# A decoder block with split fp32r weights: on-chip pools in another order, stationary high tiles 64 bytes into their slots

## The chip, the cores and the metric

The kernel runs on one core of a Trainium2 chip. The metric is device time of one execution in microseconds (us), lower is better; a profile beside it shows one execution instruction by instruction. PE is TensorE's matmul, PEld its weight load, DVE VectorE, ACT ScalarE, POOL GpSimd, SP SyncE.

## The reference

One decoder layer over 256 tokens of width 2048, all in float32: a SwiGLU feed-forward, a mixer (a gated linear recurrence beside dilated attention), a second SwiGLU, each with layer norm behind it, and a gated per-layer embedding at the end.

```python
x = layer_norm(ALPHA * x + 0.5 * swiglu(x, ffn1_w_gate, ffn1_w_up, ffn1_w_down), ln1_g, ln1_b)
mix = hybrid_mixer(x, positions, w_in, conv_w, ..., lru_lambda, w_out)
x = layer_norm(ALPHA * x + mix, ln2_g, ln2_b)
x = layer_norm(ALPHA * x + 0.5 * swiglu(x, ffn2_w_gate, ffn2_w_up, ffn2_w_down), ln3_g, ln3_b)
x = x + sigmoid(x @ w_ple_gate) * (p @ w_ple_proj)
```

## The kernel before

Weights arrive in chunks of 256 rows by 512 columns (128 partitions, two k-halves of 512, 512 KB). `make_plan` lists them in the order in which the products take them. SP loads a chunk into a `raw` tile, ACT rounds it into a `hi` tile (line 86), DVE writes the rest `raw - hi` into a `lo` tile (line 92). There are nine hi slots and nine lo slots of 4096 bytes a partition, and preparation runs up to seven chunks ahead. Activations are split in the same way; the layer's input stands transposed in `xT`, for each of 16 blocks `kb` 256 tokens of the high part and then 256 of the low part. A product is hi*hi + lo*hi + hi*lo, all through the helper `mm` (line 203). Three kinds of it fill PE, in program order:

- Gate, up and channel products (`tokens_a`, `mm_stationary_w`): the weight is stationary. For each 128x128 block of a chunk there is a pair of matmuls: the hi block with 512 columns of `xT` (both parts), then the lo block with 256 columns (the high part). A chunk has 8 pairs, a group of eight chunks 64. At the two places where a layer norm of the second token half is still due, the group runs per token half, with 256 and 128 columns.
- Down and output products (`down_mm`): the activation, in a tile of the `work` pool, is stationary; hi, lo and hi again of the weight stream past as 512 columns, in triples.
- Value, query/key and ple-gate products (`tokens_b`): the same triples with `xT` as the stationary operand. The last quarter of the ple gate (`group_b_last`) streams 256 columns for the second token half.

The first three chunks of each of three stages lie in `work` tiles instead of slots (`e["work"]`).

Each tile's place follows from the order of the pools in `build`: const (`xT`, acc, identity and tables), small, raw, hi, lo, work, work1, qk. Const takes 53,888 bytes of a partition and small 576; the raw, hi, lo and work tiles are all 4096 bytes long.

Of the kernel before, what the change touches and what calls it, by code (L numbers as in the profile page):

```python
# [6 lines left out]
F32R = mybir.dt.float32r  # L7
# [5 lines left out]
P = 128  # L13
# [5 lines left out]
QW, KVW, LRU = 1536, 512, 1536  # L19
C_X = QW + 2 * KVW  # L20
C_Y = C_X + LRU
# [9 lines left out]
MAGIC = 12582912.0  # L31
AHEAD = 7
SLOTS = 9
PI_IN = 3.1415925


class Block:
# [17 lines left out]
    def bank(self):  # L55
        return self.tile(self.psum, [P, 512], F32, "mm")

# [1 line left out]
    def split(self, hi, lo, src, pool=False):  # L59
        self.nc.scalar.copy(hi, src)  # L60
        (self.nc.gpsimd if pool else self.nc.vector).tensor_tensor(lo, src, hi.bitcast(F32), op=ALU.subtract)  # L61

# [1 line left out]
    def load(self, q):  # L64
        e = self.plan[q]
        if e.get("load"):
            e["load"]()
        e["raw"] = self.tile(self.wraw, [P, 2, 512], F32, "raw")
        for k in e["parts"]:
            self.nc.sync.dma_start(e["raw"][:, k, :], e["src"][:, k, :])  # L70

    def prepare_hi(self, q):
        while self.loaded < min(len(self.plan), q + 4):
            self.load(self.loaded)
            self.loaded += 1
        e = self.plan[q]
        if e.get("split"):
            e["split"]()
        if e["work"]:
            e["hi"], e["lo"] = self.wide_r((P, 2, 512)), self.wide_r((P, 2, 512))  # L80
        else:
            e["hi"] = self.tile(self.whi, [P, 2, 512], F32R, "hi")
            e["lo"] = self.tile(self.wlo, [P, 2, 512], F32R, "lo")
            self.live += 1
        for k in e["parts"]:
            self.nc.scalar.copy(e["hi"][:, k, :], e["raw"][:, k, :])  # L86
# [7 lines left out]
    def advance(self, need=0):  # L94
        end = min(self.limit, self.taken + AHEAD)
        while self.ready < end and (self.plan[self.ready]["work"] or self.live < SLOTS):
            self.prepare_hi(self.ready)
# [44 lines left out]
    def make_plan(self):  # L142
        i = self.i
        plan = self.plan = []

        def add(w, r0, c0, n=1, **kw):
            for j in range(n):
                plan.append({"src": self.rows2(w, r0 + 256 * j, c0), "work": False, "pool": False,
                             "parts": [slice(0, 2)], **kw})

        def ffn(name):
            g, u, d = (i[f"{name}_w_{v}"] for v in ("gate", "up", "down"))
            for c in range(NCH):
                add(g, 0, c * 512, 8)
                add(u, 0, c * 512, 8)
                if c:
                    down(d, (c - 1) * 512)
            down(d, (NCH - 1) * 512)

        def down(w, r0):  # L160
            for n in range(4):
                add(w, r0, n * 512, 2)

        w, wo = i["w_in"], i["w_out"]
        ffn("ffn1")
        for j in range(8):
            plan[j]["load"] = lambda j=j: self.load_x(j)
            plan[j]["split"] = lambda j=j: self.split_x(j)
            plan[16 + j]["load"] = lambda j=j: self.load_acc(j)
        plan[0]["parts"] = [slice(0, 1), slice(1, 2)]  # L170
        v0 = len(plan)
        add(w, 0, QW + KVW, 8)
        for g in range(3):
            add(w, 0, C_X + g * 512, 8)
        for h in range(4):
            add(w, 0, h * 512, 8)
        for g in range(3):
            add(w, 0, C_Y + g * 512, 8)
            down(wo, g * 512)
        down(wo, 3 * 512)  # L180
        f0 = len(plan)
        ffn("ffn2")
        p0 = len(plan)
        for n in range(4):
            add(i["w_ple_proj"], 0, n * 512)
        for n in range(4):
            add(i["w_ple_gate"], 0, n * 512, 8)
        for q in (v0, f0, p0):
            for e in plan[q:q + 3]:
                e["work"] = e["pool"] = True  # L190
        plan[p0]["load"], plan[p0]["split"] = self.load_p, self.split_p
        self.xraw = {}
        self.limit = len(plan)
        self.loaded = self.ready = self.ready_lo = self.taken = self.live = 0
        self.ticks = 0
        self.lru_q, self.att_q, self.gate_q, self.res_q = [], [], [], []
# [1 line left out]
    def rows2(self, w, r0, c0):  # L198
        return w[r0:r0 + 256, c0:c0 + 512].rearrange("(k p) c -> p k c", p=P)

# [1 line left out]
    def mm(self, out, lhsT, rhs, start, stop):  # L202
        self.nc.tensor.matmul(out, lhsT=lhsT, rhs=rhs, start=start, stop=stop, skip_group_check=True)  # L203

# [148 lines left out]
        for e in es[3]:  # L353
            self.done(e)

# [1 line left out]
    def ln_stats(self, st, t, n):  # L357
        self.nc.vector.bn_stats(st[:, n, :], self.acc[:, t, n * 512:(n + 1) * 512])  # L358

# [38 lines left out]
                nc.gpsimd.tensor_tensor(a, a, gb[:, 1, :], op=ALU.add)  # L398
                yield

# [1 line left out]
    def swiglu(self, boundary):  # L402
        nc = self.nc
        pend = None
        for c in range(NCH):
            gate = []

            def on_gate(b, bank):
                g = self.narrow()
                self.evac_a(bank, g)  # L410
                s = self.narrow()
                nc.scalar.activation(s, g, AF.Sigmoid)  # L412
                nc.vector.tensor_tensor(g, g, s, op=ALU.mult)  # L413
                gate.append(g)

            self.group_a(on_gate, boundary and c == 0)
            if c == 1 and not boundary:
                self.res_q.append(self.tables())
            ah, al = self.wide_r(), self.wide_r()

            def on_up(b, bank):
                u = self.narrow()
                self.evac_a(bank, u)
                nc.vector.scalar_tensor_tensor(u, gate[b], 0.5, u, op0=ALU.mult, op1=ALU.mult)  # L424
                self.split(ah[:, b, :], al[:, b, :], u)

            self.group_a(on_up)
            if pend is not None:
                self.down(pend, c == 1)
            pend = (ah, al)  # L430
        self.down_last(pend)

# [1 line left out]
    def setup(self):  # L434
        nc, i = self.nc, self.i
        c = self.const
        self.ident = c.tile([P, P], F32, name="ident")
        make_identity(nc, self.ident)
        self.mhalf = c.tile([P, 1], F32, name="mhalf")
        nc.gpsimd.memset(self.mhalf, -0.5)  # L440
        self.par = c.tile([P, 192], F32, name="par")
        self.trig = c.tile([P, 2, 2, 16], F32, name="trig")
        self.dec = c.tile([P, 2, 12], F32, name="dec")
# [11 lines left out]
    def rope_table(self):  # L455
# [13 lines left out]
        for n, part in enumerate(TWO_PI_PARTS):  # L469
            nc.vector.scalar_tensor_tensor(r, k, -part, r if n else ang, op0=ALU.mult, op1=ALU.add)  # L470
        nc.vector.tensor_scalar(r, r, PI_IN, -PI_IN, op0=ALU.min, op1=ALU.max)
        nc.scalar.activation(self.trig[:, 1], r, AF.Sin)
# [23 lines left out]
        nc.vector.tensor_scalar(self.dec[:, 0, :], h, -8.0, None, op0=ALU.mult)  # L496
        nc.vector.tensor_scalar(self.dec[:, 1, :], h, -4.0, None, op0=ALU.mult)

# [1 line left out]
    def lru(self, g, xb):  # L500
        nc, i = self.nc, self.i
        wg = self.wide((P, 2, 4, P))
# [61 lines left out]
        yield  # L564
        nc.vector.tensor_tensor(al, q, ah.bitcast(F32), op=ALU.subtract)

# [1 line left out]
    def attention(self, h, qks):  # L568
        nc = self.nc
        for t in range(2):  # L570
# [58 lines left out]
        yield  # L629
        nc.vector.tensor_tensor(self.att[1][:, h, :], ob[:, :256], self.att[0][:, h, :].bitcast(F32), op=ALU.subtract)  # L630

# [1 line left out]
    def channels(self):  # L633
        got = []

# [38 lines left out]
            act = rec  # L674
        self.down_last(act)

# [1 line left out]
    def ple_proj(self):  # L678
        nc, i = self.nc, self.i
        for n in range(4):  # L680
# [51 lines left out]
    def build(self):  # L732
        tc = self.tc
        with (
            tc.tile_pool(name="const", bufs=1) as self.const,
            tc.tile_pool(name="small", bufs=2) as self.small,
            tc.tile_pool(name="wraw", bufs=5) as self.wraw,
            tc.tile_pool(name="whi", bufs=SLOTS) as self.whi,
            tc.tile_pool(name="wlo", bufs=SLOTS) as self.wlo,
            tc.tile_pool(name="work", bufs=12) as self.work,  # L740
            tc.tile_pool(name="work1", bufs=6) as self.work1,
            tc.tile_pool(name="qkp", bufs=3) as self.qk,
            tc.tile_pool(name="psum", bufs=8, space=bass.MemoryType.PSUM) as self.psum,
            tc.manual_schedule(),
        ):
            self.xT = self.const.tile([P, KB, 2, S], F32R, name="xT")
            self.acc = self.const.tile([P, 2, D], F32, name="acc")
            self.make_plan()
            self.setup()
            self.which = 0  # L750
            self.swiglu(False)
            self.mixer()
            self.swiglu(True)
            self.ple_proj()
            self.ple_gate()
# [44 lines left out]
```

## Time and profile before

| what | value |
|---|---|
| median of three runs | 1959.88 us (1959.28 to 1960.81) |
| span of the profiled execution | 1958.6 us |
| PE busy | 1946.0 us, 99% |
| PEld busy | 1665.9 us, 85% |
| DVE, ACT busy | 1293.7 us (66%), 962.3 us (49%) |
| matmuls | 10244 |
| granted TensorE clock | 1.000 throughout |
| DMA | 375.27 MB, mean 192 GB/s |

A matmul's listed duration runs from its start to a modelled end and overlaps the next one's; what one costs in a dense stream is the distance from its start to the next start. In the timeline a row is a run of equal instructions, so the hi and the lo matmul of a pair have a row each, and a triple has one row for lo and one for two hi's.

### The profile page before, as it was taken

The numbers are of one execution on the slowest core, as the hardware profiler recorded it, in microseconds if no ns is written. First come the engines' busy times: TensorE is split into PE (matmuls) and PEld (weight loads), VectorE is DVE, ScalarE is ACT, GpSimd is POOL, SyncE is SP. The second block draws the span as 40 slices with busy tenths as digits, with TensorE's granted clock in tenths as the row PEclk, the third lists the DMA queues.
The fourth block names the chain that finished last, engine by engine and source line by source line (L and its number), as shares of the span: only waits on it lengthen the run. The fifth ranks groups of instructions, "written<-read, shape, count | busy, mean of one in ns | idle before, by whom it ended". The sixth has DMA issues, their size and how long they took to land.

```text
span 1958.6 us, 26578 instructions
## 1 busy us (share of the span) xinstructions
PE 1946.0 (99%) x10244; PEld 1665.9 (85%) x10244; DVE 1293.7 (66%) x1679; ACT 962.3 (49%) x1330; POOL 151.2 (8%) x93
## 2 busy tenths in 40 slices
PE   8999999999999999999999999999999999999999
PEld 7888888888888888888888898888888888888787
DVE  6667565656665666778677786566556656565875
ACT  6544444444444446656754545444444444444552
POOL 0000000000000012301100250000000000000151
PEclk9999999999999999999999999999999999999999
DMA  9666565556655665655456466656565656655563
GB/s 315 206 210 201 166 218 190 174 171 215 205 176 177 193 205 183 226 163 171 141 193 194 150 207 222 195 172 219 168 214 173 195 169 217 193 173 172 178 223 132
DMA packets 195007, 375.27 MB, mean 192 GB/s; under 512 B 11953, under 2 KB 14657, under 8 KB 194881
## 3 DMA queue, kind: packets, MB, share of 16 engines
q1 hardware_dynamic: 193856, 370.42, 58.4%
q0 software_dynamic: 1024, 3.16, 0.5%
q8 instruction: 80, 1.31, 0.3%
q14 instruction: 47, 0.38, 0.1%
HBM read 371.43 MB, written 2.10 MB: 191 GB/s over the span
## 4 chain that ended last, share of the span: by engine, by line
PE 99%; DVE 1%; DMA 0%; issue 0%; ACT 0%; SPq 0%; POOL 0%; DVEq 0%
PE mm L203 98%; PE mm L380 1%; DVE w L61 0%; DMA raw<-in_ffn_w_gate_dram 0%; DVE lo L92 0%; PE mm L586 0%; DVE bst L358 0%; DVE acc L315 0%; ACT hi L86 0%; POOL rs L367 0%; DVE acc L370 0%; SPq L70 0%; DVE qk L698 0%; PE mm L619 0%; PE mm L618 0%
## 5 line engine op out<-in xcount | busy, mean ns | idle before, releaser
L203 PE MATMUL mm<-xT,hi 128*128 128x512 f32 (+1 forms) x3216 | 1121.3, 393 | 6.2 <-DVE xT L61 5.3
L86 ACT CAST hi<-raw 128x1024 fp32r<-128x1024 f32 (+1 forms) x676 | 693.4, 1048 | 620.7 <-PE mm L203 423.3
L92 DVE TENSOR_TENSOR lo<-raw,hi 128x1024 fp32r<-128x1024 f32 (+1 forms) x676 | 839.5, 1280 | 231.6 <-ACT hi L86 230.1
L203 PE MATMUL mm<-xT,lo 128*128 128x256 f32 (+1 forms) x3216 | 899.1, 280 | 0.0
L203 PEld LDWEIGHTS mm<-xT,hi 128*128 128x128 f32 x3216 | 606.0, 188 | 143.6 <-ACT hi L86 6.4
L203 PEld LDWEIGHTS mm<-xT,lo 128*128 128x128 f32 x3216 | 604.1, 188 | 1.7 <-DVE lo L92 0.8
L203 PE MATMUL mm<-hi,w 128*128 128x512 f32 x1672 | 521.6, 390 | 0.0
L203 PEld LDWEIGHTS mm<-hi,w 128*128 128x128 f32 x1672 | 313.9, 188 | 65.4
L203 PE MATMUL mm<-lo,w 128*128 128x512 f32 x836 | 325.5, 389 | 0.6 <-DVE lo L92 0.6
L308 DVE TENSOR_TENSOR w<-mm,w 128x256 f32<-128x256 f32 x200 | 83.4, 419 | 194.7 <-ACT w L307 194.6
L203 PEld LDWEIGHTS mm<-lo,w 128*128 128x128 f32 x836 | 157.0, 188 | 32.7 <-DVE lo L92 1.0
L203 PE MATMUL mm<-hi,xT 128*128 128x512 f32 (+1 forms) x584 | 180.2, 385 | 0.0
L315 DVE TENSOR_TENSOR acc<-acc,mm 128x512 f32<-128x512 f32 x184 | 122.1, 681 | 63.2 <-PE mm L203 63.2
L92 POOL TENSOR_TENSOR w<-raw,w 128x1024 fp32r<-128x1024 f32 x9 | 25.9, 2911 | 1318.7 <-ACT w L86 679.8
L307 ACT COPY w<-mm 128x256 f32<-128x256 f32 x200 | 72.5, 365 | 112.3 <-PE mm L203 112.3
L203 PEld LDWEIGHTS mm<-hi,xT 128*128 128x128 f32 x584 | 107.2, 188 | 23.1
L203 PE MATMUL mm<-lo,xT 128*128 128x512 f32 (+1 forms) x292 | 111.4, 382 | 0.0
L60 ACT CAST w<-w 128x256 fp32r<-128x256 f32 x90 | 36.5, 407 | 92.3 <-DVE w L424 92.3
L61 DVE TENSOR_TENSOR w<-w,w 128x256 fp32r<-128x256 f32 x90 | 43.2, 481 | 41.9 <-ACT w L60 41.9
L413 DVE TENSOR_TENSOR w<-w,w 128x256 f32<-128x256 f32 x88 | 39.0, 444 | 44.2 <-ACT w L412 44.2
L203 PEld LDWEIGHTS mm<-lo,xT 128*128 128x128 f32 x292 | 54.8, 188 | 11.1
L412 ACT ACTIVATE w<-w 128x256 f32<-128x256 f32 x88 | 36.8, 418 | 48.6 <-DVE w L308 48.5
(125 smaller groups left out, 624.6 us busy)
## 6 DMA issues: line engine op xcount, KB each, us to landing
raw<-in_ffn_w_up_dram SPq DMA_DIRECT2D x176, 512.0 KB, 4.7
raw<-in_ffn_w_down_dram SPq DMA_DIRECT2D x176, 512.0 KB, 4.8
raw<-in_ffn_w_gate_dram SPq DMA_DIRECT2D x175, 512.0 KB, 4.6
raw<-in_w_in_dram SPq DMA_DIRECT2D x88, 512.0 KB, 4.5
raw<-in_w_out_dram SPq DMA_DIRECT2D x32, 512.0 KB, 4.6
raw<-in_w_ple_gate_dram SPq DMA_DIRECT2D x32, 512.0 KB, 4.9
w<-in_ln_g_dram SPq DMA_DIRECT2D x12, 256.0 KB, 9.0
w<-in_ln_b_dram SPq DMA_DIRECT2D x12, 256.0 KB, 7.9
```

The source lines that it names most:

```text
L60: self.nc.scalar.copy(hi, src)
L61: (self.nc.gpsimd if pool else self.nc.vector).tensor_tensor(lo, src, hi.bitcast(F32), op=ALU.subtract)
L86: self.nc.scalar.copy(e["hi"][:, k, :], e["raw"][:, k, :])
L92: eng.tensor_tensor(e["lo"][:, k, :], e["raw"][:, k, :], e["hi"][:, k, :].bitcast(F32), op=ALU.subtract)
L203: self.nc.tensor.matmul(out, lhsT=lhsT, rhs=rhs, start=start, stop=stop, skip_group_check=True)
L307: self.nc.scalar.copy(c, bank[:, 256:])
L308: self.nc.vector.tensor_tensor(dst, bank[:, :256], c, op=ALU.add)
L315: self.nc.vector.tensor_tensor(a, a, bank, op=ALU.add)
L380: nc.tensor.transpose(bank[:, q * P:(q + 1) * P], self.acc[:, t, kb * P:(kb + 1) * P], self.ident)
L412: nc.scalar.activation(s, g, AF.Sigmoid)
L413: nc.vector.tensor_tensor(g, g, s, op=ALU.mult)
```

## The change

The pools stand in another order: raw, hi, lo, work, const, small, work1, qk. A hi slot becomes 4352 bytes long; a chunk whose plan entry is marked `stationary` (gate, up, the x and y channels) begins 64 bytes into its slot, every other at the slot's start. Lo tiles, raw tiles and work tiles keep their size. The instructions, their order, shapes, waits and DMAs stay as they are. Removed comments are left out here.

```diff
+LINE = 16
...
         else:
-            e["hi"] = self.tile(self.whi, [P, 2, 512], F32R, "hi")
+            o = LINE if e["stationary"] else 0
+            e["hi"] = self.tile(self.whi, [P, 1024 + 4 * LINE], F32R, "hi")[:, o:o + 1024].rearrange("p (k c) -> p k c", k=2)
             e["lo"] = self.tile(self.wlo, [P, 2, 512], F32R, "lo")
...
-                             "parts": [slice(0, 2)], **kw})
+                             "parts": [slice(0, 2)], "stationary": False, **kw})
...
-                add(g, 0, c * 512, 8)
-                add(u, 0, c * 512, 8)
+                add(g, 0, c * 512, 8, stationary=True)
+                add(u, 0, c * 512, 8, stationary=True)
...
-            add(w, 0, C_X + g * 512, 8)
+            add(w, 0, C_X + g * 512, 8, stationary=True)
...
-            add(w, 0, C_Y + g * 512, 8)
+            add(w, 0, C_Y + g * 512, 8, stationary=True)
...
         with (
-            tc.tile_pool(name="const", bufs=1) as self.const,
-            tc.tile_pool(name="small", bufs=2) as self.small,
             tc.tile_pool(name="wraw", bufs=5) as self.wraw,
             tc.tile_pool(name="whi", bufs=SLOTS) as self.whi,
             tc.tile_pool(name="wlo", bufs=SLOTS) as self.wlo,
             tc.tile_pool(name="work", bufs=12) as self.work,
+            tc.tile_pool(name="const", bufs=1) as self.const,
+            tc.tile_pool(name="small", bufs=2) as self.small,
             tc.tile_pool(name="work1", bufs=6) as self.work1,
```

## Rows read from the trace of the kernel before

**Rows 1.** The page: an engine's busy time, share, instructions; then the chain's shares by engine.

```profile
PE 1946.0 (99%) x10244; PEld 1665.9 (85%) x10244; DVE 1293.7 (66%) x1679; ACT 962.3 (49%) x1330; POOL 151.2 (8%) x93
PE 99%; DVE 1%; DMA 0%; issue 0%; ACT 0%; SPq 0%; POOL 0%; DVEq 0%
```

**Rows 2.** Waits of PE: who waited for whom, us in total, times, longest.

```profile
PE mm L203 <- DVE xT L61: 5.3, 1, 5.3
PE mm L380 <- DVE acc L370: 1.5, 1, 1.5
PE mm L203 <- ACT hi L86: 0.9, 1, 0.9
PE mm L203 <- DVE lo L92: 0.6, 1, 0.6
```

**Rows 3.** Groups by shape: count | busy us, mean modelled ns | idle before, releaser.

```profile
L203 PE MATMUL mm<-xT,hi 128*128 128x512 f32 x3136 | 1102.3, 395 | 6.2 <-DVE xT L61 5.3 <-ACT hi L86 0.9
...
L203 PE MATMUL mm<-hi,w 128*128 128x512 f32 x1672 | 521.6, 390 | 0.0
...
L203 PE MATMUL mm<-hi,xT 128*128 128x512 f32 x520 | 169.3, 399 | 0.0
...
L203 PE MATMUL mm<-lo,xT 128*128 128x512 f32 x260 | 102.6, 395 | 0.0
...
L203 PE MATMUL mm<-xT,hi 128*128 128x256 f32 x80 | 19.1, 335 | 0.0
...
L203 PE MATMUL mm<-xT,w 128*128 128x256 f32 x48 | 11.4, 335 | 0.0
...
L203 PE MATMUL mm<-w,xT 128*128 128x512 f32 x36 | 8.9, 399 | 0.0
```

**Rows 4.** Timeline of PE, pairs behind a down stage: start, length (us), instruction.

```profile
123.82 0.28 PE L203 MATMUL mm<-xT,lo 128*128 128x256 f32 x1
...
124.17 0.28 PE L203 MATMUL mm<-xT,lo 128*128 128x256 f32 x1
...
157.66 0.28 PE L203 MATMUL mm<-xT,lo 128*128 128x256 f32 x1
```

**Rows 5.** Timeline of PE, pairs in the first group.

```profile
19.75 0.28 PE L203 MATMUL mm<-xT,lo 128*128 128x256 f32 x1
...
54.37 0.28 PE L203 MATMUL mm<-xT,lo 128*128 128x256 f32 x1
```

**Rows 6.** Timeline of PE, the first down triples behind pairs, and later ones.

```profile
166.74 0.39 PE L203 MATMUL mm<-lo,w 128*128 128x512 f32 x1
...
168.12 0.39 PE L203 MATMUL mm<-lo,w 128*128 128x512 f32 x1
...
172.20 0.39 PE L203 MATMUL mm<-lo,w 128*128 128x512 f32 x1
...
186.48 0.39 PE L203 MATMUL mm<-lo,w 128*128 128x512 f32 x1
```

**Rows 7.** Timeline of PE, query/key triples of 512 columns.

```profile
840.62 0.39 PE L203 MATMUL mm<-lo,xT 128*128 128x512 f32 x1
...
865.82 0.39 PE L203 MATMUL mm<-lo,xT 128*128 128x512 f32 x1
```

**Rows 8.** Timeline of PE, the last ple-gate triples of 256 columns.

```profile
1943.29 0.28 PE L203 MATMUL mm<-lo,xT 128*128 128x256 f32 x1
...
1953.83 0.28 PE L203 MATMUL mm<-lo,xT 128*128 128x256 f32 x1
```

**Rows 9.** Timeline of PE, pairs of a token half (256 and 128 columns).

```profile
1112.49 0.33 PE L203 MATMUL mm<-xT,hi 128*128 128x256 f32 x1
...
1115.96 0.33 PE L203 MATMUL mm<-xT,hi 128*128 128x256 f32 x1
```

**Rows 10.** Windows in a pair and a down stage: each engine's busy us, PEclk, DMA.

```profile
124.00:164.00 40.00, 40.00 (x231) 35.02 (x231) 20.66 (x23) 18.40 (x23) 0.00 (x0) 1.00 0.65 207
168.00:187.00 19.00, 19.00 (x86) 15.73 (x85) 16.16 (x22) 9.46 (x13) 0.00 (x0) 1.00 0.58 173
```

## The prediction, made before the changed kernel ran

> **What bounds the kernel now.** The page comes first. PE is busy 1946.0 of 1958.6 us, and 99% of the chain that ended last is PE [rows 1]. The waits say the same from the other side: PE waits 8.3 us in all, four waits, nearly all of it for the first tiles [rows 2]. So no other engine's work sets the end; the time is the number of matmuls times what each costs in the stream. The change leaves number, order, shapes and waits as they are, so it can move the time only through the cost of one matmul, and through that only if the places of its operands matter.
>
> The listed durations can't tell that, since they overlap. I therefore took start-to-start distances from the timeline, first against last row of a dense stretch. The counts are in [rows 3].
>
> - Pairs (512 columns with a hi block, then 256 with a lo block). Behind a down stage 33.84 us for 97 pairs, 348.9 ns a pair [rows 4]. In the first group 34.62 us for 98 pairs, 353.3 ns [rows 5]. Both cases have the same addresses, so a pair has two rhythms, and what ran before it decides which.
> - Down triples: 14.28 us for 21 triples of three 512-column matmuls, 226.7 ns each; the first two triples behind the pairs took 690 ns each, 230.0 a matmul [rows 6].
> - Triples on `xT`: 25.20 us for 36, 233.3 ns a matmul [rows 7].
> - The same with 256 columns: 10.54 us for 31, 113.3 ns a matmul, exactly half of 226.7 [rows 8].
> - Token-half pairs (256 and 128 columns): 3.47 us for 15, 231.3 ns a pair [rows 9].
>
> The reader is to see that the same 512 columns cost 226.7 or 233.3 ns with PE never idle. If every column cost what it costs in the down triples, a pair of 768 would take 1.5 x 226.7 = 340.0 ns. Pairs are 8.9 to 13.3 ns above that.
>
> **Where the operands lie.** While a matmul streams, the next one's 128x128 block is loaded, so what meets are the columns that stream and the block that is loaded. I worked out both places from the pools. Const and small take 53,888 + 576 = 54,464 bytes, 425 times 128 and 64 over. In the kernel before, raw, hi, lo and work tiles stand behind them, so all lie 64 bytes off `xT`, counted modulo 128; blocks and k-halves are 512 and 2048 bytes apart and change nothing of it. Down triples (hi or lo against work): no offset, 226.7. Triples on `xT`: 64, 233.3 at 512 columns, 113.3 (no loss) at 256. Pairs: 64 for both loads, 340.0 plus 8.9 to 13.3.
>
> After the change raw, hi, lo and work stand before `xT`; their sizes (20,480, 9 x 4352, 36,864 and 49,152) are multiples of 128. So lo, work and the unshifted hi tiles lie level with `xT`, and the shifted hi tiles 64 off.
>
> **The change part by part.**
>
> (a) Triples on `xT`: 520 + 260 + 36 matmuls of 512 columns [rows 3] go from offset 64 to none, the relation of the down triples. 816 x (233.3 - 226.7) = 5.4 us saved. From both sides: at best this, at worst nothing. I take the whole.
>
> (b) Pairs: 3136 [rows 3]. The 512-column half, under which the lo block is loaded, comes to offset 0, which at 512 columns costs nothing extra [rows 6]. The 256-column half, under which the next hi block is loaded, keeps 64, which at 256 columns cost nothing extra either [rows 8]. Each half then has the relation that is free at its length, and a pair would take 226.7 + 113.3 = 340.0. The slow rhythm holds in 11 of the 49 groups (the first four, the three x-channel groups, the first y-channel group behind the attention, the first three full ones of the second feed-forward), 704 pairs; the fast one in 38, 2432 pairs. 704 x 13.3 = 9.4 us and 2432 x 8.9 = 21.6 us, 31.0 together. The unknown is whether [rows 8] hold for a 256-column matmul between two of 512. If each load at offset 64 costs there what it costs under 512 columns, 6.7 ns [rows 6, 7], the pair is 346.7, and 704 x 6.6 + 2432 x 2.2 = 10.0 us are saved. I take 340.0, since [rows 8] have the length and the offset in question; 346.7 stays as an end of the range.
>
> (c) Token-half pairs: 80 + 48 [rows 3]. At two columns of three they would cost 170.0, but take 231.3 [rows 9], so loads bind them: two at 113.3 would be 226.7. 128 x 4.6 = 0.6 us, or nothing. I take 0.6.
>
> (d) Settling: the aligned triples lost 10 ns in each of two triples before their rhythm stood [rows 6]. Some 49 groups of pairs may each lose 20 ns when they begin: 1.0 us against the change, or nothing.
>
> (e) Down triples keep their relation: nothing. Fp32 matmuls and transposes keep theirs.
>
> (f) ACT, DVE, POOL and DMA work on shifted tiles. Their cost isn't bound by these rows, but the cover is large: in a pair stage DVE is busy 20.66 of 40 us and ACT 18.40, in a down stage, whose tiles aren't shifted among themselves, 16.16 and 9.46 of 19 [rows 10]. In 40 us 14 chunks pass, so a lo or hi pass could grow by 1.3 us before it was late. DMA moves 207 GB/s at a share of 0.65 [rows 10]; pairs 2.5% faster ask for 212. What would be late next is a chunk, and PE waits for none after the start. Nothing.
>
> **The sum.** 5.4 + 31.0 + 0.6 - 1.0 = 36.0 us off the profiled span of 1958.6 gives 1922.6; the median of the runs, 1959.88, lies 1.3 above the span, so 1923.9, said as 1924.
>
> **What the skill says against it.** The rows above show a 512-column matmul at 226.7 and at 233.3 ns with nothing else waited for. The Trainium skill, "TensorE: Matmul & The Clock Gate", Part 2 (step 1, LDWEIGHTS), states that PE reads the streaming operand and the next weights through two independent SBUF ports, and that loading weights takes no read bandwidth from the running matmul. By that rule the change does nothing. The trace doesn't bear it out as it stands, because [rows 6] and [rows 7] differ; but it doesn't refute it either, since those two differ in more than the offset.
>
> **The rivals.**
>
> *Half of it.* The 512-column halves and the triples come free, the 256-column halves pay 6.7 ns a load. For it: in the kernel before, a 256-column half sits in a lossy stream at this very offset, and rows 8 are a stream of 256 alone. Against: rows 8 are the only rows of that length and offset without another length between. 10.0 + 5.4 + 0.6 - 1.0 = 15 us saved: 1945.
>
> *Nothing happens.* The 6.7 ns belong not to the offset but to `xT` as an operand: rows 7 and both kinds of pair read it, rows 6 don't. For it: no row of before has `xT` at offset 0 in a dense stream. Against: [rows 8] read `xT` too and lose nothing. 1960, and so it would be if the modulus were another one and the offsets that arise were no better.
>
> *Slower.* The pairs fall into the slow rhythm everywhere. Place: the pair stream; mechanism: the phase between load and stream, which [rows 4] and [rows 5] show to cost 4.4 ns at the same addresses. With unlike offsets for its two loads the stream may settle nowhere, as the aligned triples do at their beginning. At 353.3 for all 49 groups: 2432 x 4.4 = 10.7 us lost, 6.0 from (a) and (c) gained, 1964.6. It decides from a mean pair of 351.8 on: today's mean is (704 x 353.3 + 2432 x 348.9) / 3136 = 349.9, and (a) and (c) pay for 1.9 ns more.
>
> **How the numbers follow.** All clean 0.5 (1921 to 1928, with (c) and (d) at their ends); half of it or between the two 0.29 (1928 to 1948); nothing 0.10 (1955 to 1962); slower 0.11 (1964 and more). The range takes the first two: 1921 to 1948, 0.79. A measurement of this kernel tells some 0.2% (4 us) from no change. Faster 0.79, same 0.10, slower 0.11.
>
> **What would show it.** Start-to-start in the timeline: pairs at 340 everywhere, in the first group too (346.7 for half of it, 349 to 353 for nothing); query/key triples at 680 a triple instead of 700; down triples unchanged at 680; token-half pairs at 227. PE's waits stay under 10 us. The forecast is wrong if pairs stand at two rhythms again, or if triples on `xT` still take 700: then the offset isn't what the loss hangs on.

## The result, and the profile after

The changed kernel takes 1930.7 us (median of four runs, 1928.07 to 1931.83), beside 1960.0 us for the kernel before on the same chip: ratio 0.9851, 95% interval 0.9837 to 0.9865. The forecast was 1924 with a range of 1921 to 1948. The sign and the range held; the time is 6.7 us above the forecast. The profiled execution has a span of 1929.2 us, 29.4 less than before.

The page after, the engines' busy time and the chain's shares, to be laid beside [rows 1]:

```profile
PE 1916.6 (99%) x10244; PEld 1654.4 (86%) x10244; DVE 1290.9 (67%) x1679; ACT 961.8 (50%) x1330; POOL 151.1 (8%) x93
...
PE 99%; DVE 1%; DMA 0%; issue 0%; ACT 0%; SPq 0%; POOL 0%; DVEq 0%
```

The waits of PE after (who waited for whom, us in total, times, longest), to be laid beside [rows 2]:

```profile
PE mm L205 <- DVE xT L62: 5.0, 1, 5.0
PE mm L382 <- DVE acc L372: 1.5, 1, 1.5
PE mm L205 <- ACT hi L88: 1.0, 1, 1.0
PE mm L205 <- DVE lo L94: 0.6, 1, 0.6
```

PE still sets the end, with the same number of matmuls and the same four waits, 8.1 us in all. PE's busy time fell by 29.4 us, exactly what the span lost. So the whole gain is in what a matmul costs in the stream, and there it must be looked for, from start to start.

The timeline of PE after (start in us, listed length, instruction): pairs behind a down stage, then pairs of the first groups, then pairs of the second feed-forward's first groups. Each shows the first and the last of 98 lo matmuls in a row.

```profile
123.86 0.28 PE L205 MATMUL mm<-xT,lo 128*128 128x256 f32 x1
...
156.84 0.28 PE L205 MATMUL mm<-xT,lo 128*128 128x256 f32 x1
...
19.91 0.28 PE L205 MATMUL mm<-xT,lo 128*128 128x256 f32 x1
...
53.86 0.28 PE L205 MATMUL mm<-xT,lo 128*128 128x256 f32 x1
...
1139.82 0.28 PE L205 MATMUL mm<-xT,lo 128*128 128x256 f32 x1
...
1173.78 0.28 PE L205 MATMUL mm<-xT,lo 128*128 128x256 f32 x1
```

Behind the down stage 32.98 us for 97 pairs, 340.0 ns, where [rows 4] gave 348.9. In the first groups 33.95 us for 97, 350.0 ns, where [rows 5] gave 353.3; and 350 again where the second feed-forward begins. The reader is to see two rhythms at the same addresses, as before the change, but 340 and 350 instead of 349 and 353. The 340.0 is the time that the prediction took for two free halves; below it is called the free rhythm.

The same view of the other products: down triples, triples on `xT`, the last ple-gate triples of 256 columns, and token-half pairs.

```profile
169.79 0.39 PE L205 MATMUL mm<-lo,w 128*128 128x512 f32 x1
...
183.39 0.39 PE L205 MATMUL mm<-lo,w 128*128 128x512 f32 x1
...
834.99 0.39 PE L205 MATMUL mm<-lo,xT 128*128 128x512 f32 x1
...
849.95 0.39 PE L205 MATMUL mm<-lo,xT 128*128 128x512 f32 x1
...
1915.72 0.28 PE L205 MATMUL mm<-lo,xT 128*128 128x256 f32 x1
...
1924.36 0.28 PE L205 MATMUL mm<-lo,xT 128*128 128x256 f32 x1
...
1095.45 0.34 PE L205 MATMUL mm<-xT,hi 128*128 128x256 f32 x1
...
1098.44 0.33 PE L205 MATMUL mm<-xT,hi 128*128 128x256 f32 x1
```

- Down triples: 13.60 us for 20, 680 ns a triple, as in [rows 6].
- Triples on `xT`: 14.96 us for 22, 680 ns, where [rows 7] gave 700.
- Last ple-gate triples: 8.64 us for 24, 360 ns, 120.0 a matmul, where [rows 8] gave 113.3. These got slower.
- Token-half pairs: 2.99 us for 13, 230.0 ns, where [rows 9] gave 231.3.

The other engines, in the two windows of [rows 10] (each engine's busy us, the granted clock, DMA share and GB/s):

```profile
124.00:164.00 40.00, 40.00 (x238) 35.48 (x237) 20.23 (x24) 18.52 (x26) 0.00 (x0) 1.00 0.63 210
168.00:187.00 19.00, 19.00 (x87) 15.80 (x86) 15.34 (x20) 10.37 (x11) 0.00 (x0) 1.00 0.69 216
```

In the pair stage more matmuls fit into 40 us (238 records against 231), DVE and ACT are as busy as before (20.2 and 18.5 us), and the granted clock is 1.00, its upper level, as before.

### The profile page after: what moved, and what is told of

Same layout as the page of the kernel before. It is cut to its first block, busy times and chain, and to the rows that moved or that the text cites. A ratio compares the mean times of both kernels' runs of the same rounds, so it can differ in the third digit from the quotient of the medians.

```text
span 1929.2 us, 26578 instructions
## 1 busy us (share of the span) xinstructions
PE 1916.6 (99%) x10244; PEld 1654.4 (86%) x10244; DVE 1290.9 (67%) x1679; ACT 961.8 (50%) x1330; POOL 151.1 (8%) x93
## 4 chain that ended last, share of the span: by engine, by line
PE 99%; DVE 1%; DMA 0%; issue 0%; ACT 0%; SPq 0%; POOL 0%; DVEq 0%
PE mm L205 98%; PE mm L382 1%; DVE w L62 0%; DMA raw<-in_ffn_w_gate_dram 0%; DVE lo L94 0%; PE mm L588 0%; DVE bst L360 0%; DVE acc L317 0%; ACT hi L88 0%; POOL rs L369 0%; DVE acc L372 0%; SPq L71 0%; PE mm L620 0%; PE mm L619 0%; SPq L713 0%
## 5 line engine op out<-in xcount | busy, mean ns | idle before, releaser
L205 PE MATMUL mm<-xT,hi 128*128 128x512 f32 (+1 forms) x3216 | 1096.0, 390 | 6.1 <-DVE xT L62 5.0
L205 PE MATMUL mm<-xT,lo 128*128 128x256 f32 (+1 forms) x3216 | 887.6, 276 | 0.0
```

## The experiments

Each is the changed kernel with one edit, if nothing else is said. Times are medians; ratios are against runs of the kernel before on the same chip, with a 95% interval. Lines from a timeline are the first and the last of a row of equal matmuls, and "each" is the distance from one to the next. "Offset" is where the loaded block begins less where the stream begins, in bytes, counted modulo 256, as it follows from the order and sizes of the pools; of a pair's two offsets the first is that of the lo block, loaded under the 512 columns, the second that of the hi block, loaded under the 256. In the triples on `xT` the loaded block lies in `xT`, so there the offset was 64 before and is 0 after.

### Only the pools in another order

```diff
-            o = LINE if e["stationary"] else 0
+            o = 0
```

> The new pool order without the 64 bytes: every tile that meets another lies level with it (offset 0 modulo 128). Length theory (a load is free at offset 0 under 512 columns and at offset 64 under 256 columns, and costs 6 to 7 ns otherwise): down triples and triples on xT stay at 680 ns, a pair is 226.7 + 120 = 346.7 or a little more, because the last ple-gate triples of the changed kernel, 256 columns at offset 0, take 120 ns a matmul; 1931 + 2516 x 6.7 = 1948 us. Level-is-good theory (offset 0 is free at every length, the 64 bytes do nothing): pairs as in the changed kernel, 1931 us.

1965.02 us (1964.46 to 1966.96), ratio 1.0028, interval 1.0017 to 1.0039: slower than before, where the expectation had 1948 or 1931. Its timeline of PE: pairs behind a down stage, pairs of the first groups, triples on `xT`, last ple-gate triples.

```profile
123.81 0.28 PE L205 MATMUL mm<-xT,lo 128*128 128x256 f32 x1
...
157.73 0.28 PE L205 MATMUL mm<-xT,lo 128*128 128x256 f32 x1
...
19.82 0.28 PE L205 MATMUL mm<-xT,lo 128*128 128x256 f32 x1
...
53.80 0.28 PE L205 MATMUL mm<-xT,lo 128*128 128x256 f32 x1
...
849.65 0.39 PE L205 MATMUL mm<-lo,xT 128*128 128x512 f32 x1
...
861.89 0.39 PE L205 MATMUL mm<-lo,xT 128*128 128x512 f32 x1
...
1952.03 0.28 PE L205 MATMUL mm<-lo,xT 128*128 128x256 f32 x1
...
1958.87 0.28 PE L205 MATMUL mm<-lo,xT 128*128 128x256 f32 x1
```

The triples on `xT` are at 680 ns (12.24 us for 18) and the last ple-gate triples at 360 (6.84 for 19): both follow from the order alone. The pairs are at 353.3 (33.92 for 96) behind the down stage and at 346.7 (33.98 for 98) in the first groups. So offset 0 is not good in itself: it is free under 512 columns and costs under 256. That each load is priced by its own offset and length has the signs right, but a price per load would make every pair 346.7, and most are 353.3. The pair has a rhythm of its own.

### Only the 64 bytes

The old order of the pools, with the longer hi slot and `o = LINE` for stationary chunks.

```diff
+            tc.tile_pool(name="const", bufs=1) as self.const,
+            tc.tile_pool(name="small", bufs=2) as self.small,
             tc.tile_pool(name="wraw", bufs=5) as self.wraw,
...
-            tc.tile_pool(name="const", bufs=1) as self.const,
-            tc.tile_pool(name="small", bufs=2) as self.small,
```

> The old pool order with the 64 bytes: the stationary hi blocks come level with xT (offset 0), the lo blocks and the triples on xT stay at 64. Length theory: both loads of a pair are at the wrong offset, so a pair is at least 233.3 + 120 = 353.3 ns, the triples on xT stay at 700; 1960 + 2432 x 4.4 = 1971 us. Level-is-good theory: only the lo load costs, a pair is 346.7, 1950 us. Placement theory (what gains is that xT lies behind the weights, not the offset): as before, 1960 us.

1958.95 us (1958.28 to 1960.06), ratio 0.9997, interval 0.9987 to 1.0006: no change. Pairs behind a down stage:

```profile
124.01 0.28 PE L205 MATMUL mm<-xT,lo 128*128 128x256 f32 x1
...
157.95 0.28 PE L205 MATMUL mm<-xT,lo 128*128 128x256 f32 x1
```

33.94 us for 97 pairs, 349.9 ns; the last ple-gate triples stay at 340 (8.84 us for 26). Counted modulo 128, the shift puts both of a pair's loads on the side that costs at their length (64 under 512, 0 under 256), yet the pair costs no more than before. That was a miss for a sum of prices, which gave 1971. The expectation's 1960 for a gain that lies in the order itself fits this run; the padded order below speaks against it. The hi tiles lie here as far from their raw and lo tiles as in the changed kernel, so that distance alone, which ACT and DVE meet when they write them, isn't where the gain comes from. Neither half of the change is worth anything alone: one loses 5 us, the other nothing, and together they gain 29.

### The order with the old offsets

A tile of 64 bytes ahead of `xT` gives all operands the offsets of the kernel before, in the new order.

```diff
-            o = LINE if e["stationary"] else 0
+            o = 0
...
+            self.pad = self.const.tile([P, 16], F32, name="pad")
```

> The new pool order, no shift of the hi tiles, and a 64-byte pad ahead of xT in const, so that every load meets its stream at the same offset as in the kernel before, while the pools stand in the new order. Offset theory: pairs at 348.9 and 353.3 ns, triples on xT at 700, 1960 us. Placement theory (the order itself matters): pairs as in the run of the new order alone, 346.7 to 353.2, triples on xT at 680, 1965 us, or anything else.

1959.73 us (1958.72 to 1960.08), ratio 1.0002, interval 0.9992 to 1.0011. Pairs behind a down stage:

```profile
123.86 0.28 PE L205 MATMUL mm<-xT,lo 128*128 128x256 f32 x1
...
157.70 0.28 PE L205 MATMUL mm<-xT,lo 128*128 128x256 f32 x1
```

33.84 us for 97 pairs, 348.9 ns, the rhythm of [rows 4]; the first groups at 353.3 as in [rows 5], triples on `xT` at 700. `xT` and the weight tiles stand tens of kilobytes from where they were, and the times are those of the kernel before. So what counts of the order is the offset that it sets: the 64 bytes of the pad alone move the time from 1965.0 to 1959.7.

### Another offset for the hi tiles: 32, 128, 192

```diff
-            o = LINE if e["stationary"] else 0
+            o = 8 if e["stationary"] else 0
```

and the same with 32 and 48 elements.

> The changed kernel with the stationary hi tiles 32 instead of 64 bytes into their slots. If what counts is which half of 128 bytes a tile begins in, this is the new order alone (353.2 and 346.7 ns a pair, 1965 us); if it counts how far apart stream and load are, something between the new order alone and the changed kernel, 1931 to 1965 us.

> The changed kernel with the stationary hi tiles 128 instead of 64 bytes into their slots. If offsets count modulo 128, this is the new order alone: pairs at 353.2 and 346.7 ns, 1965 us. If they count modulo 256 or more, the pairs take another time, and 340 is possible.

> The changed kernel with the stationary hi tiles 192 bytes into their slots. If offsets count modulo 128, this is the changed kernel: pairs at 340 and 350 ns, 1931 us. If they count modulo 256, another time; the length theory has no number for it, but a load at 192 under 256 columns is half of what the kernel before had, so up to 353 ns a pair, 1960 us.

32 bytes: 1958.85 us, ratio 0.9997 (0.9987 to 1.0007). 128 bytes: 1962.2, 1.0016 (1.0006 to 1.0027). 192 bytes: 1927.71, 0.9839 (0.9819 to 0.9859). The timelines of PE, pairs behind a down stage, first with 32:

```profile
123.75 0.28 PE L205 MATMUL mm<-xT,lo 128*128 128x256 f32 x1
...
157.81 0.28 PE L205 MATMUL mm<-xT,lo 128*128 128x256 f32 x1
```

With 128:

```profile
124.04 0.28 PE L205 MATMUL mm<-xT,lo 128*128 128x256 f32 x1
...
157.84 0.28 PE L205 MATMUL mm<-xT,lo 128*128 128x256 f32 x1
```

With 192, there and at the beginning of the second feed-forward:

```profile
124.02 0.28 PE L205 MATMUL mm<-xT,lo 128*128 128x256 f32 x1
...
157.00 0.28 PE L205 MATMUL mm<-xT,lo 128*128 128x256 f32 x1
...
1139.86 0.28 PE L205 MATMUL mm<-xT,lo 128*128 128x256 f32 x1
...
1173.81 0.28 PE L205 MATMUL mm<-xT,lo 128*128 128x256 f32 x1
```

351.1 ns a pair (34.06 for 97), 352.1 (33.80 for 96), 340.0 (32.98 for 97), and 350.0 where the second feed-forward begins (33.95 for 97). 64 and 192 bytes give the free rhythm, 0 and 128 don't, nor does 32. Counting modulo 128 sorts the good from the bad, as the prediction did, but is not the whole of it. With 128 the pairs run at 352 where the order alone had 353.3 and 346.7, and the kernel takes 1962.2 us, not the 1965 expected. And 192 is better than 64 where other work breaks into the pairs. In the last x-channel group, behind such a break, first the changed kernel, then 192 bytes:

```profile
805.85 0.28 PE L205 MATMUL mm<-xT,lo 128*128 128x256 f32 x1
...
825.10 0.28 PE L205 MATMUL mm<-xT,lo 128*128 128x256 f32 x1
...
803.49 0.28 PE L205 MATMUL mm<-xT,lo 128*128 128x256 f32 x1
...
822.22 0.28 PE L205 MATMUL mm<-xT,lo 128*128 128x256 f32 x1
```

With 64 the 55 pairs take 19.25 us, 350.0 ns each; with 192 they take 18.73, 340.5. With 192 the first groups of the kernel ran at 340.0 too, in the one execution with a profile.

### Both tiles shifted

Hi and lo tiles begin 64 bytes into slots of 4224 bytes. The slots are an odd multiple of 128 bytes apart, so the offset of successive chunks goes to and fro between 64 and 192 (0 and 128 for chunks that aren't shifted). Nine such slots leave 128 over, so a chunk's lo tile is always on the other side than its hi tile: in a triple, which streams hi, lo and hi, the offset changes at each matmul.

```diff
-            e["hi"] = self.tile(self.whi, [P, 1024 + 4 * LINE], F32R, "hi")[:, o:o + 1024].rearrange("p (k c) -> p k c", k=2)
-            e["lo"] = self.tile(self.wlo, [P, 2, 512], F32R, "lo")
+            e["hi"] = self.tile(self.whi, [P, 1024 + 2 * LINE], F32R, "hi")[:, o:o + 1024].rearrange("p (k c) -> p k c", k=2)
+            e["lo"] = self.tile(self.wlo, [P, 1024 + 2 * LINE], F32R, "lo")[:, o:o + 1024].rearrange("p (k c) -> p k c", k=2)
```

> The new pool order, and both the hi and the lo tile of a stationary chunk 64 bytes into its slot, so that a pair's two loads have the offset modulo 128 that they had before, while the triples on xT are level. Slots are 4224 bytes, so modulo 256 the offset changes from slot to slot between 64 and 192. Length theory with a modulus of 128: pairs at 349 to 353 ns as before, triples on xT at 680; 1960 - 5.4 = 1955 us. If the modulus were 256, pair times would change from chunk to chunk. Placement theory: 1931 us.

1971.79 us (1971.07 to 1972.44), ratio 1.006, interval 1.0045 to 1.0075: the slowest of all. Pairs and then down triples:

```profile
124.05 0.28 PE L205 MATMUL mm<-xT,lo 128*128 128x256 f32 x1
...
157.74 0.28 PE L205 MATMUL mm<-xT,lo 128*128 128x256 f32 x1
...
168.23 0.40 PE L205 MATMUL mm<-lo,w 128*128 128x512 f32 x1
...
185.54 0.40 PE L205 MATMUL mm<-lo,w 128*128 128x512 f32 x1
```

350.9 ns a pair on average (33.69 for 96); down triples 692.4 (17.31 for 25) instead of 680. The expectation was a miss, since it counted modulo 128, by which the triples' offset would not have changed at all. A price of 128 under 512 columns alone doesn't explain it: in the first nine down stages the matmuls that stream a tile at 128 take 230.8 ns on average, and those at 0 take 231.1, where constant offsets gave 226.7. That the changing offset never lets the stream settle would fit, but no run here separates it from a cost that spreads over the neighbours.

### Matmuls added ahead of the slow stretches

The free rhythm is absent where the first feed-forward starts and where the second takes over from token-half pairs. Eight 512-column matmuls with `xT` as both operands, so at an offset free at that length, were put ahead of the second group of either feed-forward. Their result is not used.

```diff
+    def settle(self, n):
+        bank = self.bank()
+        for _ in range(n):
+            self.mm(bank, self.xT[:, 1, 0, :P], self.xT[:, 0].rearrange("p s t -> p (s t)"), True, True)
...
+            if c == 0:
+                self.settle(8)
```

> The changed kernel with eight added level matmuls of 512 columns (their result is not used) before the second group of pairs of either feed-forward. Rhythm theory (a pair stream keeps the rhythm in which it starts, and level 512-column matmuls bring it to the free one): groups two to four of the first and the first three full ones of the second feed-forward go from 350 to 340 ns a pair, 6 x 64 x 10 = 3.8 us less for 16 x 0.227 = 3.6 us more, 1930 to 1931 us. If something else of these stretches slows the pairs (other engines, DMA), they stay at 350 and the time is 1934 us.

> As the run with eight added level matmuls, but with two at each of the two places: 4 x 0.227 = 0.9 us more. If two are enough to bring the pairs from 350 to 340 ns, up to 3.8 us less, 1928 us; if it takes the six that the down triples take to settle, the groups behind them stay at 350 and the time is 1931 to 1932 us.

Eight: 1930.57 us (1929.94 to 1931.25), ratio 0.985 (0.9835 to 0.9865). Two: 1929.06 (1928.24 to 1929.91), 0.9846 (0.983 to 0.9862). With eight, the second feed-forward's first groups:

```profile
1139.94 0.28 PE L205 MATMUL mm<-xT,lo 128*128 128x256 f32 x1
...
1172.92 0.28 PE L205 MATMUL mm<-xT,lo 128*128 128x256 f32 x1
```

With two, the first group of the kernel up to the last pair ahead of the added matmuls, and then from the first pair behind them:

```profile
13.96 0.28 PE L205 MATMUL mm<-xT,lo 128*128 128x256 f32 x1
...
30.62 0.28 PE L205 MATMUL mm<-xT,lo 128*128 128x256 f32 x1
...
31.44 0.28 PE L205 MATMUL mm<-xT,lo 128*128 128x256 f32 x1
...
73.78 0.28 PE L205 MATMUL mm<-xT,lo 128*128 128x256 f32 x1
```

340.0 ns where the changed kernel had 350 (32.98 for 97), with no address changed: what runs ahead of a stretch of pairs sets its rhythm. It works the other way too. In the run with two the first group went at 340.0 (16.66 for 49), and right behind the two added matmuls, without a wait of PE, the pairs went at 349.9 (42.34 for 121). That is one execution; with eight, the groups behind stayed at 340. That first group ran at 340 in both these executions, before anything had been added to the stream, and at 350 in the changed kernel's. To see whether that differs from execution to execution, the changed kernel ran again without an edit.

> The changed kernel once more, unedited. Rhythm theory, with the start left to chance (the first groups begin behind waits for DMA): the first four groups stand at 350 ns as in its first profile or at 340 as in the two runs with added matmuls, and everything behind them is as in the first profile; 1929 or 1931 us. If the rhythm is fixed by the program alone, they stand at 350 again.

1932.11 us. Its first groups:

```profile
20.04 0.28 PE L205 MATMUL mm<-xT,lo 128*128 128x256 f32 x1
...
53.95 0.28 PE L205 MATMUL mm<-xT,lo 128*128 128x256 f32 x1
```

33.91 us for 96 pairs, 353.2 ns, where the first execution had 350.0, and 350.0 again where the second feed-forward begins. So the start's rhythm isn't even fixed for one program. With four groups of 64 pairs at stake, 13 ns between the extremes are 3.4 us, nearly the 3.8 between the fastest and the slowest of the changed kernel's four runs; whether that is what sets these apart isn't shown, since one of the four has a profile.

### The best of it together

192 bytes for the hi tiles, and two added matmuls in the second feed-forward only.

```diff
-            o = LINE if e["stationary"] else 0
+            o = 48 if e["stationary"] else 0
...
+            if c == 0 and boundary:
+                self.settle(2)
```

> The hi tiles 192 bytes into their slots, and two added level matmuls before the second group of pairs of the second feed-forward alone. If these two bring its first three full groups from 350 to 340 ns, as they did with 64 bytes, 1.9 us less for 0.5 us more than the run with 192 bytes: 1926 to 1927 us where the first stretch runs at 340. If the phase they leave is a lossy one for 192 bytes, the groups stay at 350 and the time is 1928 us.

1925.26 us (1924.99 to 1927.89), ratio 0.9827, interval 0.9813 to 0.984: below both kernels. The second feed-forward's first groups:

```profile
1140.06 0.28 PE L205 MATMUL mm<-xT,lo 128*128 128x256 f32 x1
...
1173.04 0.28 PE L205 MATMUL mm<-xT,lo 128*128 128x256 f32 x1
```

340.0 ns (32.98 for 97), and 340.0 in the first groups as well. With nearly every pair in the free rhythm the time comes within 1.3 us of the forecast, so the pairs left at 350 are where most of the forecast's missing microseconds were.

### All offsets side by side

| kernel | lo under 512, hi under 256 | ns a pair, by stretch |
|---|---|---|
| before; order with old offsets | 192, 192 | 348.9; 353.3 |
| only the 64 bytes | 192, 0 | 350; 351; 346.7 |
| only the order | 0, 0 | 353.3; 346.7 |
| 32 bytes | 0, 32 | 351 |
| changed | 0, 64 | 340; 350 (353 at one start) |
| 128 bytes | 0, 128 | 352 |
| 192 bytes | 0, 192 | 340; 350 |
| both tiles | 64, 192 and 192, 64, to and fro | 350 to 352 (mean of a group) |

## Why the prediction was right, and where its sum was off

The sum promised 36.0 us off the profiled span; 29.4 came. Term by term:

- **What bounds the kernel.** Right: PE's busy time and the span fell by the same 29.4 us, and PE's waits stayed at 8 us.
- **(a) Triples on `xT`.** The price was right: in long stretches 700 became 680 a triple. The order alone does it, and its padded version undoes it. Its extent was not: added up from start to start over the traces, these triples gained 4.5 us, not 5.4. Many stand in stretches of 6 to 48 matmuls between other work, and most of these gained 1 to 6 ns a matmul, where the long stretches gained 6.5. The step charged settling to the pairs alone.
- **(b) Pairs.** Again the price was right and its extent was not. 340.0 is what a pair costs in most stretches, so the choice of [rows 8] as the price of a 256-column half held. But the step assumed one rhythm for all 3136 pairs. The trace shows some 570 at about 350: the first four groups (256), the three full ones at the start of the second feed-forward (192), and some 120 of the x-channel groups' end and the first y-channel group, where other work interrupts the pairs. 570 x 10 = 5.7 us not gained. All of these stretches were already in the prediction's own list of slow groups; [rows 4] and [rows 5] had shown that a pair has two rhythms at the same addresses, and the step then let that vanish.
- **(c) Token-half pairs.** They stand in one group only, the first of the second feed-forward. 231.3 became 230.0, not 226.7: 0.1 us instead of 0.6.
- **(d) Settling.** The first pair behind a down stage or a triple takes 354 ns, 14 more than the next ones. 22 groups begin so, 0.3 us instead of 1.0; a group right behind another loses nothing. With (b) that leaves 25.0 of 31.0 us for the pairs, and from start to start the traces give 25.1.
- **A term left out.** The last ple-gate part was the free case of [rows 8] because it stood at 64; the new order puts it at 0, and 32 triples of three 256-column matmuls went from 113.3 to 120.0: 96 x 6.7 = 0.6 us lost. The prediction used these rows as a price and forgot that the change moves them too.
- **(e), (f).** Right: down triples at 680, DVE and ACT as busy as before in the same windows.

From start to start, the pairs' 25.1 with their settling, 4.5 + 0.1 - 0.6 = 29.1 us in all; PE's first matmul began 0.2 us sooner in the profile after. Measured are 29.4.

The prediction named pairs at two rhythms as a sign that it is wrong, and the pairs do stand at two, 340 and 350. Its price of 340 holds for more than four pairs of five, which is why the time came out near the forecast all the same; that one rhythm holds everywhere is wrong.

Of the rivals, *half of it* falls with 340.0 in the long stretches. *Nothing happens* falls twice: `xT` is still an operand of the triples that went to 680, and the padded order, whose tiles lie elsewhere but at the old offsets, has the old time. Only places differ between the changed kernel and the one with the order alone, and they take 1930.7 and 1965.0 us. The Trainium skill, "TensorE: Matmul & The Clock Gate", Part 2 (step 1, LDWEIGHTS), states that the stream and the next weights are read through two independent ports, so that a load takes nothing from the running matmul; these two times don't bear that out as a rule for every pair of places. *Slower* was right in that the addresses don't fix the rhythm; this cost 5.7 us of gain instead of the whole. That the order alone has most pairs at 353.3, and 1965.0 us against this rival's 1964.6, is a coincidence: the rival was stated for other offsets.

**What stays open.** Why 512 columns want the load at offset 0 and 256 columns want it at 64 or 192; by what modulus (128 sorts good from bad, but the rhythms at 0 and 128 differ); why 64 and 192 differ where other work breaks into the pairs; and what sets the rhythm at the start, which differs between executions of one program. The runs show that the relation of the two places matters and that preceding matmuls choose the rhythm. They don't show the mechanism.

## What to carry to other kernels

When PE never waits, take the distance from start to start for each kind of matmul: if the same shape has two values, look at where the loaded block and the streaming columns lie relative to each other before looking anywhere else. Treat that relation as something to set for each kind of product: the best offset depends on the columns streamed, and both halves of an alternating pair must be right at once before anything is gained. If a dense stream has two rhythms at the same addresses, count in the forecast the stretches that begin behind other work at the slow one, and try a few cheap matmuls ahead of them.

## What the runs showed of the hardware that was not expected

- A move of 64 bytes in the hi tiles of the stationary chunks, at the same order of pools, is worth 34 us (1965.0 to 1930.7).
- Two matmuls more make later pairs faster (350 to 340 ns, second feed-forward) or slower (340 to 350, first one, in its one traced execution), with no address changed.
- One program started in the rhythm of 350.0 in one execution and of 353.2 in another.
- Down triples took 692.4 ns with slots of 4224 bytes, where the offset changes within each triple, and 680 with slots a multiple of 256 apart. The matmuls at either offset were slower, 231 ns against 226.7.
- Behind a break by other work the pairs come back to 340.5 ns with the hi tiles at 192, and stay at 350.0 with 64.
